# Rotary weight columns out of the shared weight buffers, and a new order of loads at the start of the latent attention

## The chip, the cores and the metric

The kernel runs on one core of one Trainium2 chip. The metric is the device time of one execution in microseconds (us), lower being better. Times are medians of several runs. The stages below are told in microseconds from the start of the profiled execution's span.

## The reference

One layer of a hybrid encoder is computed for a prompt of 1024 tokens and a sample of 32 tokens, all in 32-bit floats. What matters for the change is the mixer:

```
p = h @ w_in                                   # [q latent 384 | kv latent 256 | rotary key 32 | q_b k_b v_b | gates]
q = rms_norm(q_lat) @ w_uq                     # 8 heads of 64 + 32 columns, the 32 rotated
k_rope = apply_rope(k_r);  c_kv = rms_norm(c_kv)
k_nope, v = c_kv @ w_uk, c_kv @ w_uv           # the sample has 512 cached latents ahead of its own
o_a = softmax(mask((q_nope k_nope + q_rope k_rope) * scale)) v    # latent attention
o_b = stick-breaking attention(q_b, k_b, v_b)
merged = sigmoid(g_a) * (o_a @ w_proj_a) + sigmoid(g_b) * (o_b @ w_proj_b)
```

Then come the output projection, residual and norm, and a convolutional feed-forward part.

## The kernel before

Matrix products keep accuracy by splitting every 32-bit operand into a high part, made by ScalarE (ACT; `hi`, L65), and the difference, made by VectorE (DVE; `lo`, L68). Each product is then three matmuls on TensorE (PE): high by high, low by high and high by low (`mm3`, L72 to L74). Weights come through `wload` (L82): SyncE's queue (SP) loads a raw tile into a buffer of the tag `wr`, of which there are two, and the split writes one of two `wh` and one of two `wl` buffers. A load waits until the buffer's last readers are done.

The stages run one after the other: norm and projections, stick-breaking attention (`stage_sb`, which leaves its outputs in four DRAM tensors `ob`), latents (`stage_lat`), latent attention (`stage_mla`), merge, feed-forward up and down. Within a stage a scheduler orders the instructions of each engine, each engine executes its list in order, and SP and GpSimd (POOL) issue their DMAs in order. Inside the attention of each head pair the order of PE, ACT and DVE is written out by hand (`ORDER_A`).

`stage_lat` first makes the two key/value latent tiles (tag `lt`), then the three query latent tiles (`lat`), 128 columns each, by three products for each of eight blocks of the hidden state. Between them PE transposes the cached rotary keys, loaded by L1020, at L1024, and the key/value latents for the output at L1005, copied by ACT at L1007 and stored by POOL. Last come the rotary key columns: 32 columns of `w_in`, loaded by `wload` into a `wr` buffer, multiplied without a split at L1056, rotated with tables (L1047, L1048) and copied to the key rows by POOL (L1068). The query latents' inverse root is made by `lat_rstd`: ACT and DVE work on one row of it (an `A` tile), POOL writes it to DRAM (`lr`, L944) and reads it back as a broadcast to all partitions (`big<-lr`, L946).

`stage_mla` starts with the expansion of head pair 0: `w_uq` and `w_uk` in one `wr` tile, `w_uv` in the next. PE makes the keys (KH, KL), the values `V` (evicted by ACT at L1197 and DVE at L68), then the queries of two heads. DVE multiplies the query table `qt` by the broadcast root (L1215) and each query bank by `qt` (L1143); ACT and DVE split the result into QH and QL. The scores are L1245 to L1250. Work of another kind fills PE's gaps: `proj_b`, the projection of the stick-breaking outputs. Its operands are the four `ob` tensors, loaded in two halves (L1471) into four `A` tiles and split into `ObH` and `ObL`; its weights are `w_proj_b` tiles through `wr`. The cached latents go into the tile `VSm` (L1104) and are first read by transposes at L1341, at the start of head pair 1.

Of the kernel before, what the change touches and what calls it, by code (L numbers as in the profile page):

```python
# [8 lines left out]
F32 = mybir.dt.float32  # L9
# [8 lines left out]
P = 128  # L18
D = 1024
KT = 8  # L20
TP = 1024
# [11 lines left out]
BIG = 1056  # L33
# [3 lines left out]
HC = 528  # L37
# [7 lines left out]
class K:  # L45
# [920 lines left out]
    def stage_lat(self):  # L966
        nc, a = self.nc, self.a
# [12 lines left out]
        lp = self.tc.alloc_tile_pool(name="lt", bufs=2, reuse_waits="tile")  # L980
# [11 lines left out]
        def ckv_out():  # L992
            for k in range(2):
                self.hi(self.CPh[k], fc[k][:, :TP])
                self.lo(self.CPl[k], fc[k][:, :TP], self.CPh[k])
                nc.vector.tensor_copy(self.CN[:, k * TS : k * TS + TS], fc[k][:, TP:T])
            for t0 in (0, 4, 8):
                st = self.tl(self.At, [P, TP], F32, "A")
                for t in (t0, t0 + 2)[: 2 - t0 // 8]:
                    tr = self.bank("tr")  # L1000
                    r, n = (P, 2) if t < 8 else (TS, 1)
                    for j in range(n):
                        for k in range(2):
                            x = fc[k][:, (t + j) * P : (t + j) * P + r]
                            nc.tensor.transpose(tr[:r, j * 256 + k * P : j * 256 + k * P + P], x, self.idt)  # L1005
                    c = (t - t0) * 256
                    nc.scalar.copy(st[:r, c : c + n * 256], tr[:r, : n * 256])  # L1007
                if t0 < 8:
                    nc.gpsimd.dma_start(a["ckv_p"][0, 0, t0 * P : (t0 + 4) * P].rearrange("(j r) c -> r j c", r=P),
                                        st.rearrange("r (j c) -> r j c", j=4))  # L1010
                else:
                    nc.gpsimd.dma_start(a["ckv_s"][0, 0], st[:TS, :256])
# [15 lines left out]
        for m in range(3):  # L1028
            wh, wl = self.w_in_tile(m * P)
            g = self.gvT[:, 16 + m : 17 + m]  # L1030
            for c0, n, ps in self.mtile(wh, wl, self.Hh, self.Hl, self.BLK, KT, "mm s s"):
                c, ps = slice(c0, c0 + n), ps[:, :n]
# [5 lines left out]
                    nc.vector.tensor_tensor(sq[:, c], sq[:, c], d, ALU.add)  # L1038
            if m == 1:
                ckv_out()  # L1040
        raw = self.wload([(0, 256, a["w_in"][0, :, 640:672].rearrange("(k p) c -> p k c", p=P), 8)])
        wk = raw[:, 0:256].rearrange("p (k c) -> p k c", k=8)
        rot = self.tl(self.At, [P, BIG], F32, "big")
        cc, ss, kr, sw = (rot[:, q * TQ : q * TQ + TQ] for q in range(4))
        for q in range(4):
            r, c = slice(32 * q, 32 * q + 32), slice(TQ * q, TQ * q + TQ)
            nc.sync.dma_start(cc[r], a["k_ropek"][0:32, c])  # L1047
            nc.sync.dma_start(ss[r], a["k_ropek"][64:96, c])  # L1048
        ps = self.bank("mm")[:, :TQ]
# [15 lines left out]
        for r in halves:  # L1065
            for q in range(4):
                w = min(TQ, TP - TQ * q)
# [23 lines left out]
    def stage_mla(self):  # L1091
        nc, a = self.nc, self.a

        O = self.Op = self.tc.alloc_tile_pool(name="mlo", bufs=2, side="right", reuse_waits="tile")
# [6 lines left out]
        Vs = None  # L1101
        self.KSm = self.tl(M, [P, 2, KS], F32, "KSm")
        self.VSm = self.tl(M, [P, 5, 256], F32, "VSm")
        nc.sync.dma_start(self.VSm[:, :4], a["cache_mla_ckv"][0, 0].rearrange("(t p) c -> p t c", p=P))  # L1104

        def expansion(p, banks="mm"):

# [76 lines left out]
        def values(hf, raw, gt):  # L1184
# [3 lines left out]
            for t in range(0, 8, 2):  # L1188
# [7 lines left out]
                for q in range(2):  # L1196
# [6 lines left out]
        load_values = lambda hf: self.wload([(0, 512, a["w_uv"][0, :, hf * 256 : hf * 256 + 256]  # L1203
                                              .rearrange("(k p) c -> p k c", p=P), 2)])
        proj = self.proj_b(M, AB)
        steps, QH, QL = expansion(0, "mm s s")
        raw = load_values(0)
        steps["I"]()
# [23 lines left out]
        for p in range(4):  # L1232
# [45 lines left out]
            U = proj["U"]  # L1278
# [30 lines left out]
        for k in ks:  # L1309
            f = self.tl(self.At, [P, BIG], F32, "big")  # L1310
# [4 lines left out]
        raw = self.tl(M, [P, 2, KS], F32, "KSm")  # L1315
        raw = [self.w_proj_a(m, raw[:, m, :512]) for m in range(2)] + [self.w_proj_a(2)]
        self.w2 = raw[2]
        for m, tags in enumerate(("mm mm s", "s s")):
            h, l = self.split_proj(raw[m])
# [138 lines left out]
    def proj_b(self, M, AB):  # L1458

        nc, a = self.nc, self.a  # L1460
        HB = HC // 2
        TILES = ((0, 1), (1, 2), (3, 1), (4, 1), (5, 2), (7, 1))
        raw, w, ps, ob, done = [], [], [], [], [0, 0]

        def operands():
            h = done[0] // 6
            ob[:] = [self.tl(M, [P, 4, HC], F32R, g) for g in ("ObH", "ObL")]
            for k in range(4):
                f = self.tl(self.At, [P, BIG], F32, "big") if h else self.tl(self.At, [P, TP], F32, "A")
                f = f[:, :HC]  # L1470
                nc.sync.dma_start(f, self.obd[k][:, h * HC : h * HC + HC])  # L1471
                self.hi(ob[0][:, k], f)
                self.lo(ob[1][:, k], f, ob[0][:, k])

        def load():
            m, n = TILES[done[0] % 6]
            done[0] += 1
            raw.append(self.wload([(0, n * 512, a["w_proj_b"][0, :, m * P : (m + n) * P].rearrange("(k p) c -> p k c", p=P), 4)]))

        def high():  # L1480
            i = done[1] % 6
            done[1] += 1
            n = TILES[i][1] * 512
            w.append([x[:, :n] for x in AB[i % 3 != 1]])
            self.hi(w[-1][0], raw[0][:, :n])

        def low():
            x = raw.pop(0)
            self.lo(w[-1][1], x[:, : w[-1][1].shape[-1]], w[-1][0])

        def steps():
            for h in range(2):
                for m, i in ((m, i) for m, n in TILES for i in range(n)):
                    if i == 0:
                        wh, wl = (x.rearrange("p (k c) -> p k c", k=4) for x in w.pop(0))
                    m, d = m + i, slice(i * P, i * P + P)
                    for c0 in (0, HB):
                        c = slice(c0, c0 + HB)
                        ps.append((m, h * HC + c0, self.bank("mm")[:, :HB]))
                        for k in range(4):  # L1500
                            self.mm3(ps[-1][2], wh[:, k, d], wl[:, k, d], ob[0][:, k, c], ob[1][:, k, c], k == 0, k == 3)
                            yield

        def store():
            m, c0, x = ps.pop(0)
            g = self.tl(self.At, [P, 512], F32, "nat")[:, :HB]
            nc.scalar.copy(g, x)
            nc.gpsimd.dma_start(self.pbd[m, :, c0 : c0 + HB], g)

        step = steps()  # L1510
        return dict(O=operands, U=load, W=high, w=low, f=lambda: next(step), G=store)


    def natural(self, facc, lhs, ws, first, done=None, sample=None, tiles=range(8)):
# [825 lines left out]
```

## Time and profile before

| | |
|---|---|
| median of 3 runs | 1711.94 us (1710.65 to 1712.59) |
| profiled execution | 1715.34 us, span 1713.6 us |
| granted TensorE clock | 0.995 |
| PE, DVE, ACT, POOL busy | 98%, 72%, 57%, 16% of the span |
| latents, head pair 0 begins | about 512 to 594, then from 595 us |

In the rows of a timeline the columns are start, duration, engine, line, operation, tiles written and read, and shapes; in brackets stand the engine's idle time before the instruction and what ended it. `x3` after a row means that three neighbours are merged into it. The waits view gives, for an engine and a line, what it waited for: sum in us, times, longest. A row of groups gives busy time and mean duration (ns) of the instructions of one form. A row of DMA issues gives the count, the size of each and the median time from issue to landing. Matmuls overlap in their pipeline, so the time of one counts from start to start.

### The profile page before, as it was taken

To read this page: it belongs to the slowest core of one execution; us is meant where nothing else is said; L and a number is where in the kernel's file an instruction comes from. 1 tells how busy PE (TensorE), PEld (TensorE's weight loads), DVE (VectorE), ACT (ScalarE), POOL (GpSimd) and SP (SyncE) were. 2 spreads that over 40 slices of the span, in tenths; PEclk is the share of its full clock that TensorE was granted. 3 is DMA by queue.
4 is the path that set the end of the run, shared out by engine and by line. 5 is a ranking of instruction groups with operands and counts; after the bars stand their busy time and mean duration, and the time that the engine had idled before them with its cause. 6 is when DMAs were issued, how large, how long until landed. Compare 5 with 4: busy or idle time off the path is not lost. (4 is left out here: it accounts for less than half of the span.)

```text
span 1713.6 us, 29725 instructions
## 1 busy us (share of the span) xinstructions
PE 1674.5 (98%) x11526; PEld 1524.6 (89%) x11526; DVE 1236.0 (72%) x2065; ACT 979.1 (57%) x1902; POOL 277.6 (16%) x530
## 2 busy tenths in 40 slices
PE   6999999999999999999999999999999999999998
PEld 3899999999999889988889789999999999977886
DVE  4596595593782488877775779887787787788456
ACT  4495595693773467777673376544444444545442
POOL 2211111111110121111000121221121111110013
PEclk8999999999999999999999999999999999999999
DMA  9244342333441231222174631523323333697753
GB/s 328 83 117 121 94 131 78 98 107 86 140 123 48 89 101 53 67 59 74 52 272 150 191 123 36 168 93 130 130 93 130 130 105 130 224 332 248 230 151 120
DMA packets 169805, 224.33 MB, mean 131 GB/s; under 512 B 13326, under 2 KB 115872, under 8 KB 169664
## 3 DMA queue, kind: packets, MB, share of 16 engines
q1 hardware_dynamic: 153216, 177.11, 32.9%
q0 software_dynamic: 16224, 45.24, 7.6%
q8 instruction: 90, 1.47, 0.4%
q14 instruction: 51, 0.42, 0.1%
q10 hardware_dynamic: 224, 0.09, 0.0%
HBM read 170.34 MB, written 51.25 MB: 129 GB/s over the span
## 5 line engine op out<-in xcount | busy, mean ns | idle before, releaser
L65 ACT ACTIVATE wh<-wr 128x1024 fp32r<-128x1024 f32 (+5 forms) x153 | 130.6, 861 | 247.9 <-PE s L1794 82.2
L68 DVE TENSOR_TENSOR wl<-wr,wh 128x1024 fp32r<-128x1024 f32 (+5 forms) x153 | 150.4, 989 | 137.8 <-ACT wh L65 135.3
L72 PE MATMUL mm<-hh,wh 128*128 128x352 f32 x688 | 229.5, 334 | 2.2 <-ACT nat L870 2.2
L73 PE MATMUL mm<-hl,wh 128*128 128x352 f32 x688 | 223.9, 325 | 0.4 <-DVE hl L300 0.3
L74 PE MATMUL mm<-hh,wl 128*128 128x352 f32 x688 | 223.2, 324 | 0.0
L72 PEld LDWEIGHTS mm<-hh,wh 128*128 128x128 f32 x688 | 129.8, 189 | 10.2 <-ACT nat L870 4.1
L73 PEld LDWEIGHTS mm<-hl,wh 128*128 128x128 f32 x688 | 129.8, 189 | 3.5 <-DVE hl L300 2.1
L74 PEld LDWEIGHTS mm<-hh,wl 128*128 128x128 f32 x688 | 129.9, 189 | 0.4 <-issue 0.4
L1795 PE MATMUL s<-T,wl 128*128 128x256 f32 (+1 forms) x328 | 93.6, 285 | 0.0
L1794 PE MATMUL s<-T,wh 128*128 128x256 f32 (+1 forms) x328 | 93.4, 285 | 0.0
L1793 PE MATMUL s<-T,wh 128*128 128x256 f32 (+1 forms) x328 | 93.3, 284 | 0.0
L1934 DVE SCALAR_TENSOR_TENSOR u<-u,c,u 128x1058 f32<-128x1058 f32 x68 | 87.0, 1317 | 2.0 <-ACT u L1931 0.7
L611 PE MATMUL tr<-c,A 128*128 128x128 f32 x576 | 83.5, 273 | 0.5 <-DVE A L727 0.3
L1793 PE MATMUL tr<-T,wh 128*128 128x272 f32 (+1 forms) x272 | 77.8, 286 | 0.0
L1795 PE MATMUL tr<-T,wl 128*128 128x272 f32 (+1 forms) x272 | 77.6, 285 | 0.1
L1794 PE MATMUL tr<-T,wh 128*128 128x272 f32 (+1 forms) x272 | 77.3, 284 | 0.0
L68 DVE TENSOR_TENSOR wl<-S,wh 128x1024 fp32r<-128x1024 f32 x40 | 48.9, 1224 | 36.7 <-ACT wh L65 35.5
L611 PEld LDWEIGHTS tr<-c,A 128*128 128x128 f32 x576 | 67.8, 140 | 6.3 <-ACT A L550 1.6
L1795 PE MATMUL mm<-T,wl 128*128 128x256 f32 (+1 forms) x256 | 72.9, 286 | 0.3 <-DVE wl L68 0.2
L1793 PE MATMUL mm<-T,wh 128*128 128x256 f32 (+1 forms) x256 | 73.0, 285 | 0.0
L1794 PE MATMUL mm<-T,wh 128*128 128x272 f32 (+1 forms) x256 | 72.7, 284 | 0.0
L68 DVE TENSOR_TENSOR PTl<-tr,PTh 128x512 fp32r<-128x512 f32 x96 | 64.6, 684 | 8.2 <-ACT PTh L65 7.9
(694 smaller groups left out, 5444.1 us busy)
## 6 DMA issues: line engine op xcount, KB each, us to landing
wr<-in_w_ada_dram SPq DMA_DIRECT2D x48, 512.0 KB, 4.3
wr<-in_w_up_dram SPq DMA_DIRECT2D x44, 512.0 KB, 3.9
dr<-in_w_down_dram SPq DMA_DIRECT2D x43, 512.0 KB, 5.1
wr<-in_w_in_dram SPq DMA_DIRECT2D x33, 512.0 KB, 4.8
wr<-gdn SPq DMA_DIRECT2D x30, 512.0 KB, 4.9
gdn<-u POOLq DMA_DIRECT2D x23, 512.0 KB, 5.4
gd<-nat POOLq DMA_DIRECT2D x48, 176.0 KB, 2.1
t<-gd SPq DMA_DIRECT2D x16, 528.0 KB, 5.5
```

What stands on the lines that cost most here:

```text
L65: self.nc.scalar.activation(out, in_, AF.Identity, scale=scale)
L68: return self.nc.vector.tensor_tensor(out, full, hi.bitcast(F32), ALU.subtract)
L72: m(ps, lh, rh, start=start, stop=False)
L73: m(ps, lh, rl, start=False, stop=False)
L74: self.pe = m(ps, ll, rh, start=False, stop=stop).ins
L611: self.nc.tensor.transpose(tr[:, (2 * s + q) * P : (2 * s + q + 1) * P], at[q][:, b * P : b * P + P], self.idt)
L1793: m(ps[:, :n], w[0][:, k], x[0][:, k, c], start=first and k == 0, stop=False, skip_group_check=True)
L1794: m(ps[:, :n], w[0][:, k], x[1][:, k, c], start=False, stop=False, skip_group_check=True)
L1795: i = m(ps[:, :n], w[1][:, k], x[0][:, k, c], start=False, stop=k == 3, skip_group_check=True)
L1934: nc.vector.scalar_tensor_tensor(y, u[:, w : w + YW], self.cvT[:, w, cc : cc + 1], y, ALU.mult, ALU.add)
```

## The change

The rotary columns get a tile of their own, `wk`, in the stage's own pool `lt`, in place of a `wr` buffer. In `stage_mla` the loads of the first halves of the stick-breaking outputs become a function of their own (`fetch`, key `P`), called before the expansion; the cached latents' load is written behind it, with the condition that it is not issued before the last of those four loads. `operands` splits what `fetch` has loaded, and calls it where that has not happened, as for the second halves.

```diff
-        raw = self.wload([(0, 256, a["w_in"][0, :, 640:672].rearrange("(k p) c -> p k c", p=P), 8)])
-        wk = raw[:, 0:256].rearrange("p (k c) -> p k c", k=8)
+        wk = lp.tile([P, 8, 32], F32, name=self.nm("wk"), bufs=1)
+        nc.sync.dma_start(wk, a["w_in"][0, :, 640:672].rearrange("(k p) c -> p k c", p=P))
...
-        nc.sync.dma_start(self.VSm[:, :4], a["cache_mla_ckv"][0, 0].rearrange("(t p) c -> p t c", p=P))
...
         proj = self.proj_b(M, AB)
+        proj["P"]()
+        with self.tc.issue_after(self.fetched):
+            nc.sync.dma_start(self.VSm[:, :4], a["cache_mla_ckv"][0, 0].rearrange("(t p) c -> p t c", p=P))
         steps, QH, QL = expansion(0, "mm s s")
...
-        raw, w, ps, ob, done = [], [], [], [], [0, 0]
-
-        def operands():
+        raw, w, ps, ob, fs, done = [], [], [], [], [], [0, 0]
+
+        def fetch():
             h = done[0] // 6
-            ob[:] = [self.tl(M, [P, 4, HC], F32R, g) for g in ("ObH", "ObL")]
             for k in range(4):
                 f = self.tl(self.At, [P, BIG], F32, "big") if h else self.tl(self.At, [P, TP], F32, "A")
-                f = f[:, :HC]
-                nc.sync.dma_start(f, self.obd[k][:, h * HC : h * HC + HC])
+                fs.append(f[:, :HC])
+                self.fetched = nc.sync.dma_start(fs[-1], self.obd[k][:, h * HC : h * HC + HC]).ins
+
+        def operands():
+            ob[:] = [self.tl(M, [P, 4, HC], F32R, g) for g in ("ObH", "ObL")]
+            if not fs:
+                fetch()
+            for k in range(4):
+                f = fs.pop(0)
                 self.hi(ob[0][:, k], f)
                 self.lo(ob[1][:, k], f, ob[0][:, k])
...
-        return dict(O=operands, U=load, W=high, w=low, f=lambda: next(step), G=store)
+        return dict(P=fetch, O=operands, U=load, W=high, w=low, f=lambda: next(step), G=store)
```

In the built program the instructions of both kernels are the same in number. What differs in their order: on SP, the rotary columns' load stands ahead of the last query latent tile's, `w_uq` and `w_uk` ahead of the cached rotary keys, and the four `ob` loads ahead of the cached latents; on ACT and DVE, the splits of `ob` stand earlier among the copies of `V`; on PE, the transposes at L1024 stand two products later; on POOL, one copy of key rows (L1225) stands one store earlier. Everything from head pair 0's scores on stands in the same order.

## The prediction, made before the changed kernel was run

> **What bounds the kernel now.** I read the page's first part, then the waits of PE in the stretch that holds the change (540 to 625 us), then SP's queue there, then the timelines of ACT, DVE and PE row by row.
>
> ```profile
> PE 1674.5 (98%) x11526; PEld 1524.6 (89%) x11526; DVE 1236.0 (72%) x2065; ACT 979.1 (57%) x1902; POOL 277.6 (16%) x530
> ```
> ```profile
> PE tr L1005 <- ACT A L1007: 1.2, 1, 1.2
> PE s L72 <- DVE V L68: 0.9, 1, 0.9
> PE s L1250 <- DVE QL L68: 0.9, 1, 0.9
> PE s L1245 <- DVE big L1143: 0.4, 1, 0.4
> PE s L1245 <- ACT QH L65: 0.3, 1, 0.3
> ```
>
> PE is busy for 98% of the span, so an edit gains only where PE stands still, and loses only where it makes PE stand still. The second fence is the waits view for PE between 540 and 625 us (sum, count, longest): five waits, 3.7 us together. Nothing else in this stretch stops PE, so these five are the whole prize. None names a DMA. The next rows show that a DMA stands behind every one: SP's queue first.
>
> ```profile
> 550.06 0.37 SPq L82 DMA_DIRECT2D wr<-in_w_in_dram  x1
> 551.03 0.92 SPq L1020 DMA_DIRECT2D nat<-in_cache_mla_krope_dram  x2
> 570.46 0.39 SPq L82 DMA_DIRECT2D wr<-in_w_uq_dram  x1
> 578.10 0.37 SPq L82 DMA_DIRECT2D wr<-in_w_uv_dram  x1
> 588.74 0.37 SPq L82 DMA_DIRECT2D wr<-in_w_proj_b_dram  x1
> 594.81 0.37 SPq L1104 DMA_DIRECT2D VSm<-in_cache_mla_ckv_dram  x1
> 595.27 0.46 SPq L82 DMA_DIRECT2D wr<-in_w_proj_b_dram  x1
> 595.83 1.95 SPq L1471 DMA_DIRECT2D A<-ob  x4
> ```
> ```profile
> 573.52 0.69 ACT L65 ACTIVATE wh<-wr 128x576 fp32r<-128x576 f32 x1 [3.96 <-DMA wr<-in_w_uq_dram]
> 574.89 1.07 ACT L1007 COPY A<-tr 128x512 f32<-128x512 f32 x2
> 601.37 0.39 ACT L1197 ACTIVATE V<-mm 128x256 fp32r<-128x256 f32 x1
> 604.49 0.65 ACT L65 ACTIVATE ObH<-A 128x528 fp32r<-128x528 f32 x1 [1.93 <-DMA A<-ob]
> 607.67 0.65 ACT L65 ACTIVATE ObH<-A 128x528 fp32r<-128x528 f32 x1 [1.41 <-DMA A<-ob]
> ```
>
> The load at 550.06 brings the rotary columns into one of the two `wr` buffers, where they stay until the rotary products (L1056) end at 594.8. Everything else goes through the other buffer, one at a time: `w_uq` at 570.46, `w_uv` at 578.10, the first `w_proj_b` tile at 588.74. The second `w_proj_b` tile needs the rotary buffer (595.27). The cached latents' load (594.81) needs memory that the same products read. The four loads of the stick-breaking outputs (`ob`) stand behind both. ACT is in order: it waits 3.96 us for `w_uq`, then 1.93 and 1.41 us for `ob`, with the copies that PE needs queued behind.
>
> **Part 1: the rotary columns leave the `wr` pool.** In the built program their load stands ahead of the last query-latent tile's and waits only for attention products that are over before the latents begin; `w_uq` and `w_uk` take the place at 550.06, so the 3.96 us wait goes. What is late next is ACT's `wh` buffer, which the products of the second query-latent tile read until just before these transposes:
>
> ```profile
> 572.31 1.03 PE L1005 MATMUL tr<-c,lt 128*128 128x128 f32 x8
> 575.53 1.15 PE L1005 MATMUL tr<-c,lt 128*128 128x128 f32 x8 [1.22 <-ACT A L1007]
> ```
>
> So ACT's split starts at 572.4 instead of 573.52, and the copy at 574.89, three instructions behind it, 1.1 us earlier. PE waited 1.22 us for that copy and then waits 0.1. Worth 1.1 us (bounds 0 and 1.2).
>
> What is put in the way: 416 KB (288 + 128) instead of 128 KB are now queued right ahead of the two key loads (L1020), whose transposes PE runs here:
>
> ```profile
> 554.36 0.63 PE L1024 MATMUL tr<-c,nat 128*128 128x128 f32 x4
> ```
> ```profile
> wr<-in_w_uq_dram SPq DMA_DIRECT2D x1, 288.0 KB, 3.0
> A<-ob SPq DMA_DIRECT2D x4, 264.0 KB, 9.5
> big<-lr POOLq DMA_DIRECT2D x1, 528.0 KB, 8.1
> big<-lr POOLq DMA_DIRECT2D x1, 528.0 KB, 4.2
> ```
>
> The `w_uq` load took 3.0 us to land, so from 550.06 it lands at 553.1. The key loads were issued by 551.95 and landed by 554.36, within 2.4 us. At worst they begin when `w_uq` has landed: 555.5, or 1.1 us late. The new PE order sets the transposes two products later, 0.3 us at the 0.17 of the products further below (27 from 609.52 to 613.96), so PE loses at most 0.8. At best nothing changes, as the rotary load of 128 KB also stood ahead before. I take 0.3, nearer the free end, since the key loads are issued a microsecond behind either way. The Trainium skill ("DMA: Bandwidth & Descriptors", section on queues, rings and completion order) says that each DMA engine consumes one queue's descriptors in ring order. By that rule the cost is the 0.8 end and the sum below is 3.8 us instead of 4.3; no view here separates the two.
>
> **Part 2: the `ob` loads go ahead.** The second `w_proj_b` tile now waits for DVE's split of `w_uv`. In the kernel before, the load at 588.74 waits for that same split, so the tile leaves at 588.74 less the 1.1 of part 1, at 587.6. Three `ob` loads follow at once, done by 589.5; their buffers were last read by the latents' output stores, done long before. At the crowded 9.5 us they land by 599.0. The fourth waits until the 4 KB root row has been written, which is what POOL also waits for here:
>
> ```profile
> 596.17 0.57 POOL L946 DMA_DIRECT2D big<-lr  x1 [1.32 <-DMA lr<-A]
> ```
>
> That makes it 595.1. The broadcast `big<-lr` (528 KB) and the cached latents (512 KB) then travel beside it, instead of those two, three more `ob` loads and a `w_proj_b` tile. The two `big<-lr` rows give the price of a crowd: 4.2 us alone, 8.1 within it. With the lighter crowd I take the middle, 6, so the fourth lands at 601. The cached latents are late by nothing: their first reader is L1341, in the second head pair. The loads behind them on SP wait for later splits anyway. On POOL one copy of key rows (L1225) moves ahead of one store; the second head's scores read it, after the whole first head.
>
> Now DVE, the engine behind four of the five waits:
>
> ```profile
> 600.91 0.42 DVE L68 TENSOR_TENSOR V<-mm,V 128x256 fp32r<-128x256 f32 x1
> 610.24 1.25 DVE L1215 TENSOR_TENSOR qt<-qt,big 128x1056 f32<-128x1056 f32 x1
> ```
> ```profile
> L68 DVE TENSOR_TENSOR ObL<-A,ObH 128x528 fp32r<-128x528 f32 x4 | 2.8, 706 | 2.0 <-ACT ObH L65 1.8
> L1143 DVE TENSOR_TENSOR big<-s,qt 128x352 f32<-128x352 f32 x4 | 2.1, 518 | 0.0
> L68 DVE TENSOR_TENSOR KL<-A,KH 64x1024 fp32r<-64x1024 f32 x1 | 1.2, 1223 | 0.0
> ```
>
> From the first V difference to the query table's product (L1215) DVE takes 9.3 us for eight V differences (0.42) and four ObL (0.71): 6.2 us of work, the rest waiting for ACT. ACT's own part is eight copies (0.39), four ObH (0.65) and a weight split of an ObH's length, 6.4 us begun before DVE's, so it keeps pace. Starting at 600.91 - 1.1 = 599.8, the table product starts at 606.0 instead of 610.24: 4.2 earlier. It also needs `big<-lr`: 595.1 + 6 = 601 (603.2 at 8.1).
>
> ```profile
> 608.11 0.49 PE L1074 MATMUL tr<-c,big 128*128 128x128 f32 x3
> 609.52 0.40 PE L72 MATMUL s<-lat,wh 128*128 128x352 f32 x1 [0.93 <-DVE V L68]
> 613.96 0.32 PE L74 MATMUL s<-lat,wl 128*128 128x352 f32 x1
> 614.54 0.39 PE L1245 MATMUL s<-KH,QH 128*128 128x256 f32 x1 [0.26 <-ACT QH L65]
> 616.03 0.39 PE L1250 MATMUL s<-KH,QL 128*128 128x256 f32 x1 [0.90 <-DVE QL L68]
> 616.80 0.39 PE L1245 MATMUL s<-KH,QH 128*128 128x256 f32 x1 [0.38 <-DVE big L1143]
> 617.66 0.44 PE L1245 MATMUL s<-KH,QH 128*128 128x384 f32 x1
> 618.42 0.28 PE L72 MATMUL mm<-ObH,wh 128*128 128x264 f32 x1
> ```
>
> First stall: three transposes at a tenth each (eight took 1.03) would let the second head's queries start at 608.5; they start at 609.52, held by the seventh of the eight V differences. All eight are now done by 606.0, before PE comes by at 607.4. Worth 1.0.
>
> Second stall: the last query product starts at 613.96, the next could at 614.1. Three score groups follow, and the filler starts at 618.42: 4.3 us. The third group (384 columns) took 0.76 to the next start; at that pace 256 + 256 + 384 columns take 1.8. So 2.5 are lost (1.5 by the waits view alone, since a stall also shows the pipeline's fill). In the changed kernel PE reaches the scores at about 612. DVE's queue up to QL is, from 606.0: table 1.25, weight split 0.7 (as ObL), three products with the table 1.55, KL 1.2, QL of the same length 1.2, so 611.9. It comes just in time and this wait goes. The second head's products with the table then wait only for PE, so the bank of the third score group is free as PE arrives. I take 2.5, bounds 1.0 and 2.8.
>
> **The sum.** 1.1 - 0.3 + 1.0 + 2.5 = 4.3 us. Nothing later gives it back in the trace: PE, DVE and ACT start the first head pair with the same distances to each other, and PE stays the bound. The profiled execution took 1715.34 us (span 1713.6, 1.7 around it); it would take 1711.0. The median of the runs is 1711.94, 3.4 below that execution, and becomes 1707.6. About 0.2% (3.4 us) is what a measurement of this kernel can tell from no change.
>
> **Rivals.**
> *A, only part arrives.* ACT and DVE get rid of the DMA waits, but QL and the table products still end behind PE. DVE's sum of 611.9 against PE's 612 has no slack, which speaks for it; that 612 is PE's earliest, with no stall on the way, speaks against. The scores then give 1.0 instead of 2.5 and the key loads cost 0.8: 1.1 - 0.8 + 1.0 + 1.0 = 2.3, or 1709.6.
> *B, the fourth `ob` load takes the place.* Issued at 595.1, at 9.5 us it lands at 604.6, and ACT is due there by 602.5 (two V copies and three ObH, 2.7 us, behind the first V). V copies are queued behind, and the table product moves by 2.1 to 608.1: 2.1 ahead of before. Less 0.3 at L1024, 1.8 us: 1710.1. Against it: the 9.5 came with 1.3 MB more in flight (three `ob` loads and a `w_proj_b` tile).
> *C, slower.* The new ACT order has two ObH splits right behind the first V copy, ahead of the other seven; before, two more V copies came first. Were the first `ob` loads not to leave earlier (if a buffer's wait held them to 596), the second would land at 596.2 + 9.5 = 605.7, and DVE then still has 5.8 us of V and ObL work: table product at 611.5, 1.3 later than before, with 0.3 at L1024: 1713.5. It becomes a loss from a landing of 604.4 on. Against it: none of their waits ends after 589.
> *D, nothing moves*, because PE's stalls are other than named: 1711.9.
>
> **How the numbers follow.** Forecast 0.70, A 0.14, B 0.07, C 0.06, D 0.03. The forecast's own bounds: 5.0 us at most (1.2 + 1.0 + 2.8, keys free), that is 1706.9; 3.0 at least. The lowest of the three runs before lay 1.3 us below their median, so the low end is 1705.6. The high end takes in A, and B with 0.7 of the same scatter: 1710.8. Faster by over 0.2% is nearly all of the forecast and a little of A, 0.70; slower by over 0.2% at most C, 0.06; within 0.2% the rest, 0.24.
>
> **What would show it.** Right: `w_uq` issued near 550, no DMA wait on ACT's splits, `ob` loads near 588, the five waits of PE down to under 0.6 us, the filler that started at 618.42 near 614. Wrong: L1024 waiting for its load past 555; ACT waiting for the fourth `ob` load; PE still waiting for QL. A gain under 2 us with all waits gone would mean that PE's time is set elsewhere.

## The result, and the profile after

The changed kernel takes 1708.04 us (median of 22 runs, 1705.33 to 1711.15), the kernel before 1712.35 (22 runs, 1709.24 to 1716.29): a ratio of 0.9977 (95% interval 0.9971 to 0.9983), 4.3 us less. Measured twice more it came to 0.9973 (0.9963 to 0.9983) and 0.9975 (0.9965 to 0.9985). The forecast was 1707.6 us.

The first fence is the page's line of busy times. Then come the waits of PE from 540 to 625 us, one row where the kernel before had five, and SP's queue.

```profile
PE 1671.6 (98%) x11526; PEld 1524.1 (89%) x11526; DVE 1234.8 (72%) x2065; ACT 978.3 (57%) x1902; POOL 274.6 (16%) x530
```
```profile
PE tr L1024 <- DMA nat<-in_cache_mla_krope_dram: 0.3, 1, 0.3
```
```profile
549.74 0.37 SPq L82 DMA_DIRECT2D wr<-in_w_uq_dram  x1
550.16 0.48 SPq L82 DMA_DIRECT2D wr<-in_w_uk_dram  x1
550.96 0.92 SPq L1020 DMA_DIRECT2D nat<-in_cache_mla_krope_dram  x2
570.32 0.38 SPq L82 DMA_DIRECT2D wr<-in_w_uv_dram  x1
576.80 10.98 SPq L82 DMA_DIRECT2D wr<-in_w_proj_b_dram  x2
587.87 7.23 SPq L1472 DMA_DIRECT2D A<-ob  x4
595.19 0.39 SPq L1207 DMA_DIRECT2D VSm<-in_cache_mla_ckv_dram  x1
```

`w_uq` leaves at 549.74 instead of 570.46, the `ob` loads begin at 587.87 instead of 595.83, and the fourth (the row of four ends at 595.10) goes just ahead of the cached latents. The timelines of ACT and DVE show what follows.

```profile
572.22 0.69 ACT L65 ACTIVATE wh<-wr 128x576 fp32r<-128x576 f32 x1 [2.78 <-PE s L73]
598.55 1.17 ACT L65 ACTIVATE ObH<-A 128x528 fp32r<-128x528 f32 x2
600.56 1.18 ACT L65 ACTIVATE ObH<-A 128x528 fp32r<-128x528 f32 x2
```
```profile
599.56 0.42 DVE L68 TENSOR_TENSOR V<-mm,V 128x256 fp32r<-128x256 f32 x1
604.69 1.25 DVE L1217 TENSOR_TENSOR qt<-qt,big 128x1056 f32<-128x1056 f32 x1
609.22 1.21 DVE L68 TENSOR_TENSOR QL<-big,QH 128x1024 fp32r<-128x1024 f32 x1
610.71 0.52 DVE L1142 TENSOR_TENSOR big<-s,qt 128x352 f32<-128x352 f32 x1
611.15 0.51 DVE L1142 TENSOR_TENSOR big<-mm,qt 128x352 f32<-128x352 f32 x1
611.65 0.53 DVE L1142 TENSOR_TENSOR big<-s,qt 128x352 f32<-128x352 f32 x1
```

ACT's split of `w_uq` no longer waits for a DMA but for PE's release of `wh`, and the four ObH splits have no bracket: their data is there. The query table's product (now L1217) starts 5.13 us behind the first V difference instead of 9.33. On PE:

```profile
554.58 0.63 PE L1024 MATMUL tr<-c,nat 128*128 128x128 f32 x4 [0.33 <-DMA nat<-in_cache_mla_krope_dram]
572.19 1.03 PE L1005 MATMUL tr<-c,lt 128*128 128x128 f32 x8
574.24 1.14 PE L1005 MATMUL tr<-c,lt 128*128 128x128 f32 x8
606.76 0.49 PE L1074 MATMUL tr<-c,big 128*128 128x128 f32 x3
607.01 0.41 PE L72 MATMUL s<-lat,wh 128*128 128x352 f32 x1
611.29 0.32 PE L74 MATMUL s<-lat,wl 128*128 128x352 f32 x1
611.45 0.28 PE L1247 MATMUL s<-KH,QH 128*128 128x256 f32 x1
611.93 0.28 PE L1247 MATMUL s<-KH,QH 128*128 128x256 f32 x1
612.41 0.34 PE L1247 MATMUL s<-KH,QH 128*128 128x384 f32 x1
613.06 0.29 PE L72 MATMUL mm<-ObH,wh 128*128 128x264 f32 x1
```

From the first to the second row of L1005 PE needs 2.05 us, before 3.22; from the three transposes at L1074 to the second head's queries 0.25, before 1.41; from the last query product to the filler 1.77, before 4.46. To compare stretches between kernels I took the same matmuls in each trace, by their number in order of start (3602, 3735, 3887 and 4199 of 11,526, which in the first profile of before start at 549, 570, 590 and 632 us). Three profiles of each kernel (one of each comes from the first pair, the others from the experiments below):

| stretch of PE, us | before | changed | difference of means |
|---|---|---|---|
| keys transposed, 549 to 570 | 20.95, 20.62, 20.70 | 21.15, 20.98, 21.13 | +0.3 |
| latents' transposes, 570 to 590 | 20.06, 19.78, 19.58 | 18.84, 18.85, 18.84 | -1.0 |
| values, queries, scores, 590 to 632 | 41.95, 41.89, 42.10 | 37.91, 37.92, 37.93 | -4.0 |
| sum | 82.96, 82.29, 82.38 | 77.90, 77.75, 77.90 | -4.7 |

The first pair of profiles differs by 7.1 us in all (1715.34 and 1708.21). What goes beyond this stretch differs from execution to execution: the three of before took 1715.34, 1711.82 and 1710.66 us.

### The profile page after: what moved, and what is told of

It reads as the page before. It is cut to its first block, busy times and chain, and to the rows that moved or that the text cites. A ratio compares the mean times of both kernels' runs of the same rounds, so it can differ in the third digit from the quotient of the medians.

```text
span 1706.4 us, 29725 instructions
## 1 busy us (share of the span) xinstructions
PE 1671.6 (98%) x11526; PEld 1524.1 (89%) x11526; DVE 1234.8 (72%) x2065; ACT 978.3 (57%) x1902; POOL 274.6 (16%) x530
```

## The experiments

**The columns alone.** Only the first part of the diff; the cached latents' load keeps its place ahead of `ob`.

```diff
+        wk = lp.tile([P, 8, 32], F32, name=self.nm("wk"), bufs=1)
+        nc.sync.dma_start(wk, a["w_in"][0, :, 640:672].rearrange("(k p) c -> p k c", p=P))
```

> The kernel before with only the rotary columns in a tile of their own; the cached latents' load stays ahead of the ob loads. My theory (two parts, and the ob loads' departure is what matters in the second): PE's 1.22 us wait at L1005 goes, 0.2 us is lost at L1024, and no more, because the ob loads still stand behind a load that waits for the rotary products, so they leave from about 594 on, the second lands at about 603, just short of the 604.4 at which a loss begins, and the query table product starts near 609. PE still waits for V, QL and the score banks, 2.0 to 2.5 us together. Gain 0.9 us (0.3 to 1.8), about 0.05%. Rival 1 (the tile alone does it all, since it also lets the second w_proj_b tile leave early and thins the crowd): gain 4 to 5 us, 0.25 to 0.3%, the filler behind the scores starts near 613. Rival 2 (late ob loads in front of the copies of V cost): a loss of 0 to 1 us.

1709.74 us, ratio 0.9979 (0.9970 to 0.9988). By the times that is a gain of 3.6 us (2.1 to 5.1). The profile shows less where the change acts: from 549 to 632 us PE takes 80.4 us, 2.2 less than the mean of before. That is more than my 0.9 and less than rival 1. Its rows on SP, ACT and DVE:

```profile
594.81 0.37 SPq L1104 DMA_DIRECT2D VSm<-in_cache_mla_ckv_dram  x1
595.27 1.95 SPq L1471 DMA_DIRECT2D A<-ob  x4
```
```profile
599.89 1.17 ACT L65 ACTIVATE ObH<-A 128x528 fp32r<-128x528 f32 x2
604.28 0.65 ACT L65 ACTIVATE ObH<-A 128x528 fp32r<-128x528 f32 x1 [2.27 <-DMA A<-ob]
```
```profile
600.90 0.42 DVE L68 TENSOR_TENSOR V<-mm,V 128x256 fp32r<-128x256 f32 x1
608.55 1.25 DVE L1215 TENSOR_TENSOR qt<-qt,big 128x1056 f32<-128x1056 f32 x1
```

The `ob` loads do leave as late as before. But ACT splits the first two without a wait at 599.89, 4.6 us after the first was issued; only the third makes it wait. I had priced the second load at 9.5 us, the median of the row of four. The view knows the landing of the third and the fourth alone (8.8 and 10.2 us), so this was never a price of the second. So rival 2, the slower case of the prediction, starts from a wrong price: with the splits early and the loads late DVE gains 0.8 to 1.8 us (7.65 against 9.33, 8.47 and 9.49 in the profiles of before) instead of losing any. Part of that may come from the second `w_proj_b` tile, which is no longer in flight beside `ob`; with it, in the next run, the distance is 7.91.

**The order alone.** The changed kernel with the columns back in a `wr` buffer.

```diff
-        wk = lp.tile([P, 8, 32], F32, name=self.nm("wk"), bufs=1)
-        nc.sync.dma_start(wk, a["w_in"][0, :, 640:672].rearrange("(k p) c -> p k c", p=P))
+        raw = self.wload([(0, 256, a["w_in"][0, :, 640:672].rearrange("(k p) c -> p k c", p=P), 8)])
+        wk = raw[:, 0:256].rearrange("p (k c) -> p k c", k=8)
```

> The changed kernel with the rotary columns back in a wr buffer; only the order of the loads is changed. My theory: PE's 1.2 us wait at L1005 stays. The ob loads stand behind the second w_proj_b tile, which waits for the rotary buffer until 594.8, so they leave from 595.3 on, as late as before; the second lands at 603 to 604, the table product starts near 610, and the sum is 0 (between a gain of 1.0 and a loss of 1.3 us), within 0.1% of before. Rival 1 (the order of the loads brings the gain by itself, being ahead of the cached latents): gain 3 to 4 us, 0.2%. Rival 2 (the slower case of the prediction): loss of 1.0 to 1.6 us.

1711.51 us, ratio 0.9995 (0.9986 to 1.0004): no change that can be told, as expected. The wait at L1005 stays (0.9 us), and `ob` leaves behind the tile that waits:

```profile
586.46 6.89 SPq L82 DMA_DIRECT2D wr<-in_w_proj_b_dram  x2
593.45 1.90 SPq L1472 DMA_DIRECT2D A<-ob  x4
595.40 0.48 SPq L1207 DMA_DIRECT2D VSm<-in_cache_mla_ckv_dram  x1
```

The table product comes 7.91 us behind the first V difference, and PE takes 81.7 us from 549 to 632, 0.9 less than the mean of before. The parts alone give 2.2 and 0.9, together 4.7: the second needs the first, which frees the queue ahead of it. In this profile, as in one of the three of before, the granted clock fell behind the scores, which cost 0.8 us (last section). Without it the three numbers are about 1.9, 1.4 and 4.4, so some 1 us is what the parts gain only together.

**Both kernels again**, for the scatter of single profiles.

> The changed kernel once more, for a second profile. If the change's effect ends in the stretch of 540 to 625 us, the ends of PE's matmuls lie about 5 us ahead of before at 625 us in this profile too, and what is gained or lost after 700 us (2 us in the first pair of profiles) differs from execution to execution. If the change acts on the later stages, the same 2 us come back at the same places (847, 890 and 1500 to 1540 us). Median near 1708.

> The kernel before once more, for a second profile: the same five waits of PE (3.7 us in 540 to 625 us), and against the first profile of before shifts of up to 2 us after 700 us, if the later shifts are scatter between executions; shifts under 0.3 us, if they are not.

1707.88 and 1711.82 us. Of the five waits four came again; the one for V did not (the table product comes 8.47 us behind the first V difference here). The effect ends at 632 us: there the second profiles are 3.6 us apart (the changed one began the stretch 0.9 us later), and 3.9 at the end. Of the 1.8 us that the first pair gains after 700 us, 1.1 us stand between the two profiles of before as well; they belong to the first execution, not to the change.

**The cached latents from ACT's queue**, at their old place, beside the columns' tile.

```diff
-        nc.sync.dma_start(self.VSm[:, :4], ...
+        nc.scalar.dma_start(self.VSm[:, :4], ...
```

> The kernel before with the rotary columns in a tile of their own (as in the run of the columns alone) and the cached latents' load issued from ACT's queue, at its old place in the program, so that nothing that waits for the rotary products stands ahead of the ob loads on SP. The number of bytes in flight stays what it was. My theory (the second part of the gain is the place in SP's in-order queue, behind a waiting load, and nothing else): the first three ob loads leave near 588, the fourth near 595, the table product comes within 5.5 us of the first V difference (7.7 with the columns alone, 5.1 in the changed kernel), PE's waits for QL and the score banks go, and the ends of PE's matmuls gain what the changed kernel gains, 4.5 to 5.2 us, 2.3 us more than the columns alone; ratio near 0.9975. Rival (the cached latents' 512 KB beside the ob loads are what delays them): the table product stays near 7.5 us and the gain near 2.3 us.

1708.95 us, ratio 0.9981 (0.9972 to 0.9991); PE takes 79.0 us from 549 to 632, 3.5 less than before, and the table product comes at 6.04. That lies between theory and rival.

```profile
594.08 0.40 ACTq L1104 DMA_DIRECT2D VSm<-in_cache_mla_ckv_dram  x1
602.35 0.65 ACT L65 ACTIVATE ObH<-A 128x528 fp32r<-128x528 f32 x1 [0.82 <-DMA A<-ob]
```
```profile
588.48 7.41 SPq L1471 DMA_DIRECT2D A<-ob  x4
```

Three `ob` loads leave at 588.48, as in the changed kernel. The fourth leaves with 512 KB of cached latents just ahead of it on another queue, lands in 6.8 us instead of 2.7, and ACT waits for it. From 590 to 632 us PE takes 40.0 us with the columns alone (mean of two profiles), 38.6 here and 37.9 in the changed kernel: of these 2.1 us about 1.4 are the place behind a waiting load in SP's queue. The other 0.7 are lost with the cached latents ahead of the fourth load. My "nothing else" was wrong. This split rests on one profile here, and the two with the columns alone differ by 0.5 us. The times don't separate the three kernels (0.9979, 0.9981 and 0.9977 of before).

**The rotary keys from ACT's queue**, in the changed kernel.

```diff
-            nc.sync.dma_start(kr.rearrange(...
+            nc.scalar.dma_start(kr.rearrange(...
```

> The changed kernel with the two loads of the cached rotary keys (L1020) issued from ACT's queue instead of SP's, where 416 KB stand ahead of them. If those 416 KB hold them up (ring order), PE's wait at L1024 (0.3 us in the first profile of the changed kernel, its transposes 0.4 us later than in three profiles without the change) goes, and 0.3 to 0.5 us are gained there. If the wait is the keys' own time to land (2.9 us), it stays. Elsewhere nothing moves; the total is within scatter of the changed kernel either way.

```profile
549.26 0.39 ACTq L1020 DMA_DIRECT2D nat<-in_cache_mla_krope_dram  x1
549.78 0.43 ACTq L1020 DMA_DIRECT2D nat<-in_cache_mla_krope_dram  x1
553.44 0.63 PE L1024 MATMUL tr<-c,nat 128*128 128x128 f32 x4 [0.63 <-DMA nat<-in_cache_mla_krope_dram]
```

1707.22 us, a single run. The wait stays, at 0.63 us; the keys took 3.6 us to land with nothing ahead of them on their queue, against 3.0 behind the 416 KB on SP's queue in the first profile of the changed kernel. So a queue of their own doesn't bring them sooner. The Trainium skill ("DMA: Bandwidth & Descriptors", section "Issuing engines are not separate DMA queues") says that the queues of all issuing engines run on the same DMA engines and interleave; this trace agrees in so far as the other queue gained nothing (3.6 against 3.0 us).

**More work on DVE.** In the changed kernel the query table is multiplied by 1.0 two or five times more behind its product, and nothing else changes.

```diff
+        for _ in range(2):      # or 5
+            nc.vector.tensor_scalar(qt, qt, 1.0, None, ALU.mult)
```

> The changed kernel with two more products of the query table by 1.0 on DVE, right behind the table product, so that all that follows on DVE is later and nothing else changes (no DMA, no other engine). From the rows of two scalings (0.35 us for 256, 0.49 for 512 columns) each should take some 0.75 us, 1.5 together. My theory: in the changed kernel DVE's QL ends 1.3 us before PE asks for it, so only about 0.2 us (0 to 0.6) is lost at the scores. Rival (DVE's queue comes just in time, as the prediction's sum had it): 1.5 us are lost.

> The same with five more products, 3.75 us on DVE. My theory: beyond the 1.3 us of slack each us on DVE costs one us, so 2.4 us (1.9 to 3.2) are lost at the scores, PE waits for QL and the score banks as in the kernel before, and the ratio to before goes from 0.9975 to near 0.999. Rival (no slack): 3.75 us. Rival 2 (PE's stall at the scores was made by something other than DVE's queue): under 1 us.

DVE's QL is 1.56 and 3.86 us later, and PE's stretch from 590 to 632 us grows by 1.37 and 4.34. With two products a single run takes 1709.28 us. With five it is 1713.24 us and a ratio of 1.0007 (0.9998 to 1.0016): the whole gain is gone. My 1.3 us of slack was wrong, the rival without slack right. The rows with two products show where the slack went:

```profile
610.86 0.53 DVE L1142 TENSOR_TENSOR big<-s,qt 128x352 f32<-128x352 f32 x1
611.73 0.51 DVE L1142 TENSOR_TENSOR big<-s,qt 128x352 f32<-128x352 f32 x1
```
```profile
611.44 0.39 PE L1249 MATMUL s<-KH,QH 128*128 128x256 f32 x1 [0.38 <-DVE big L1142]
612.30 0.44 PE L1249 MATMUL s<-KH,QH 128*128 128x384 f32 x1
```

The second and third score groups start 0.05 and 0.06 us after the first and third of the second head's table products have ended (611.39 and 612.24): they need those banks, and the products stand behind QL in DVE's queue. In the changed kernel the third product ends at 612.18 and the third group starts at 612.41, 0.17 us more than the 0.06 that the hand-over takes. So QL has 1.3 us to spare, but what is queued behind it has 0.17. Put that way, all profiles but three lie on one line. Its last column is the time that PE would take if each us by which QL comes later than in the changed kernel, less those 0.17, cost one us:

| kernel | QL behind first V difference, us | PE, 590 to 632 us | 37.91 + (QL - 9.66 - 0.17) |
|---|---|---|---|
| changed (three profiles) | 9.66 | 37.91 to 37.93 | |
| cached latents from ACT | 10.57 | 38.63 | 38.65 |
| two more products | 11.22 | 39.28 | 39.30 |
| columns alone (two profiles) | 11.72, 12.18 | 39.78, 40.26 | 39.80, 40.26 |
| before (first, third) | 13.86, 14.02 | 41.95, 42.10 | 41.94, 42.10 |
| order alone | 12.44 | 41.33 | 40.52 |
| before (second) | 12.99 | 41.89 | 41.07 |
| five more products | 13.52 | 42.25 | 41.60 |

The last three lie 0.65 to 0.82 us above it. They are the three in which the granted clock fell behind the stalls (the last section).

**The weights behind the keys.** In the changed kernel `w_uq` and `w_uk` are held until the keys' loads are issued.

```diff
+            with self.tc.issue_after(self.keyload):
                 raw = self.wload([
...
```

> The changed kernel with the loads of w_uq and w_uk held until the two loads of the cached rotary keys have been issued, so that the 416 KB stand behind the keys instead of ahead of them; the transposes at L1024 go back to their old place, two products earlier. The run with the keys on ACT's queue left the wait in place (0.63 us), so a place in SP's queue is not what holds the keys up. Theory 1 (the 416 KB in flight share the DMA engines with the keys, whatever the queue; those that start first are served first): the keys land in the 3.05 us that they have in the kernel before, no wait at L1024, and PE takes 0.3 to 0.6 us less from 549 to 570 us than in the profiles of the changed kernel (20.98 and 21.15). Theory 2 (bytes that start behind the keys slow them as much): a wait of 0.3 to 1.0 us stays. No other stretch changes; the total is within 0.1% of the changed kernel.

> The changed kernel a third time, on the chip of the run above, for a third profile: a wait at L1024 between 0 and 1.0 us, PE's stretch from 590 to 632 us the same as in the two profiles before it (37.9 us) within 0.1 us, median near 1708.

1707.70 us, 0.9970 (0.9959 to 0.9980), and 1707.86 us, 0.9975: not to be told apart. PE takes 21.01 us from 549 to 570, against 21.15, 20.98 and 21.13 in the changed kernel. The wait for the keys is gone from the view, as theory 1 has it, but the time is not shorter. PE still stands still for 0.17 us at L1024. The view puts that down to DVE's L942, which can't be the cause: in the second profile of before the transposes started at 552.27, 0.27 us before that instruction ended.

This stretch scatters more than three profiles show. In the five other runs with the weights ahead of the keys on SP's queue it takes 21.02 to 21.80 us, though the two doses on DVE, which gave both of these ends, do not touch it. So one profile can't price the order of these loads to better than some tenths, and why PE takes 0.3 us or more beyond before there stays open.

**A third profile of before and a second of the columns alone**, for the fall of the clock.

> The kernel before a third time. In its second profile, in the run with the order alone and in the one with five more products, the granted clock falls to 0.50 for 3.4 us right behind the stalls at the scores (about 614.5 to 618.5 us) and the 15 filler products cost 1.5 us more; in the first profile of before and in the run with the columns alone the same stalls leave it at 1.00; in no profile without these stalls does it fall there. If the fall depends on how the stalls lie in time and not on the kernel, it comes or not in this profile, with PE's stretch from 549 to 632 us between 81.5 and 83.5 us; if the first profile was the exception, it comes again.

> The kernel before with the rotary columns alone, a second time, for the same question: PE's stretch from 549 to 632 us 80.4 us without a fall of the clock behind the scores, 81.9 us with one. The three gains of its first profile (1.1 us at L1005, the wait for V gone, the table product 7.7 us behind the first V difference) come again in either case.

1710.66 and 1709.41 us; the clock stays at 1.00 behind the scores in both. PE's stretch is 82.4 and 80.0 us. The fall comes and goes with the execution; the gains of the columns alone came again (wait at L1005 and wait for V gone, table product at 7.19), though the wait for V was also missing in one profile of before.

## Why the prediction was right

**The sum.** Forecast 1.1 - 0.3 + 1.0 + 2.5 = 4.3 us; the profiles give 1.0 - 0.3 + 4.0 = 4.7, the times 4.3 (2.9 to 5.0 from the interval). Of the 4.0 the first pair has 1.2 at the first stall (forecast 1.0) and 2.7 at the second (forecast 2.5). "These five are the whole prize" was wrong: the waits view gives 3.7 us, and in the first pair their places gave 5.3 (20.06 - 18.84 and 41.95 - 37.91). The distance from start to start, which the prediction used for the second stall, came closer than the waits view, which gave less than PE lost.

**Part 1.** `w_uq` left at 549.74 and ACT's split started at 572.22, released by PE (forecast 572.4). The gain was 1.0 (forecast 1.1). The cost at L1024 was 0.3 (forecast 0.3) in the three profiles of the changed kernel; in the five other runs with these loads in this order it was 0.3 to 1.0, so that this term fits so well is in part luck. Ring order as the prediction priced it did not show: the transposes started at 554.58, not at 555.5, and neither a queue of their own nor a place ahead of the weights made this stretch of PE shorter by more than 0.1 us. What the cost is made of was not found.

**Part 2, the loads.** They left as forecast (587.87 and 595.1). `big<-lr` landed in 6.2 us (forecast 6), the fourth `ob` load in 2.7 (forecast 6): with the cached latents ahead of it, in the run from ACT's queue, it took 6.8.

**Part 2, DVE.** Here a term was mis-sized. I added durations, 6.2 us for twelve differences; on DVE neighbours overlap (a V difference lasts 0.42 us, and the next instruction starts 0.33 behind it), and the twelve took 5.13 from start to start. The table product came 1.1 us sooner than my step had it, and mostly by that QL ended at 610.43, not 611.9.

**The second stall.** "It comes just in time" was right, but not for the reason given. "The second head's products with the table then wait only for PE" failed: they wait for DVE, behind QL, and their third has the 0.17 us. Had DVE really needed 6.2 us, about 0.9 us of the gain would have been lost, by the line of the table above. The two mistakes cancelled, which was luck.

**The rivals.** A, only part arrives: its waits were gone, but its condition, no slack, is what the two doses found. B: no wait for the fourth load in the changed kernel; with the cached latents in its way it waits 0.82 us, so the mechanism is real and smaller than priced. C: its situation (late `ob`, early splits) was run twice, and neither was slower (0.9979 and 0.9995 of before). Its price, 9.5 us for the second of four loads, was that of the third and the fourth. D fell with the first row of waits.

**Where the gain comes from** is told less well by the prediction's two parts than by the experiments: the columns alone bring 1.0 at L1005, lose 0.5 at L1024 and bring 1.7 to 2.2 of what I had put down to the order of the `ob` loads (two profiles).

## What to carry to other kernels

A DMA that waits for its buffer holds up all that stands behind it in its queue (the `ob` loads left at 595.27 behind one, and three of them at 588.48 without it), so ask of each late load what the one ahead of it waits for. Here two such holders had to go for the whole gain, and taking away the second alone gained nothing that the times could tell. A median over several loads is no price for the first of them. Time a chain on an in-order engine from start to start, and look past the instruction that a consumer waits for to the ones queued behind it that free the banks: the slack is the smallest of them. A small dose of work in that chain measures the slack in one run.

## What the runs showed of the hardware that was not expected

Behind the stalls at the scores the granted clock of TensorE fell to 0.50 in some executions. The windows view of the second profile of before (columns: stretch, its length, busy time of PE, PEld, DVE, ACT and POOL, granted clock, share of the DMA engines, GB/s), and below it the same stretches of the third:

```profile
612.00:615.00 3.00, 1.75 (x9) 1.16 (x10) 2.86 (x9) 0.79 (x2) 1.28 (x3) 1.00 0.50 94
615.00:618.00 3.00, 3.00 (x15) 3.00 (x15) 2.91 (x4) 1.78 (x7) 0.00 (x0) 0.50 0.00 0
```
```profile
612.00:615.00 3.00, 1.64 (x8) 1.05 (x8) 2.90 (x8) 0.81 (x1) 1.89 (x4) 1.00 0.63 131
615.00:618.00 3.00, 2.96 (x21) 2.61 (x21) 2.89 (x7) 2.80 (x8) 0.00 (x0) 1.00 0.00 0
```

With PE busy for 1.75 of 3 us the clock halved for 3.4 us (0.51, 0.50, 0.50 and 0.78 in the four stretches of 1 us from 615), and PE passed 15 matmuls where it passed 21 in the third profile; with 1.64 of 3 us it did not halve. The fall happened in one of three profiles of before, in that of the order alone and in that with five more products, never at this place in one without these stalls; it cost 0.65 to 0.82 us net in the table above.

Stretches of 3 us taken at will do not tell the cases apart; the clock's own steps do. In each of the 14 profiles any two changes of the granted clock lie a whole number of steps of 3.4133 us apart, to 0.03 us. In the second of before they are at 24.52, 27.94, 31.34, 34.76, 615.02, 618.44 and 1707.30 us. Carried on to the stalls, this grid gives the stretch at whose end the clock could change. Here are those of the second of before (the fall follows), the order alone (it follows), the columns alone and the first of before (it does not):

```profile
611.61:615.02 3.41, 2.00 (x12) 1.28 (x11) 3.27 (x10) 1.20 (x2) 1.63 (x4) 1.00 0.51 101
610.83:614.24 3.41, 2.07 (x12) 1.47 (x11) 3.28 (x9) 1.35 (x2) 2.21 (x4) 1.00 0.57 120
611.65:615.06 3.41, 2.24 (x14) 1.89 (x12) 3.29 (x7) 2.12 (x2) 2.40 (x5) 1.00 0.58 145
612.56:615.97 3.41, 2.31 (x13) 1.85 (x12) 3.35 (x5) 2.01 (x2) 3.38 (x6) 1.00 0.72 161
```

PE was busy for 1.90 to 2.07 us in the three grid stretches that a fall followed, and for 2.24 or more in those at the scores of all other profiles. Each profile of before has some 3.41 us at the stalls with only 1.8 of work; whether a stretch of the grid takes in so little depends on where the grid lies. That is how the same stalls bring a fall in one execution and none in the next. Busy time is not the whole rule: near the start of the third profile of before the stretch from 19.41 us has 1.92, and no fall followed.

The Trainium skill ("TensorE: Matmul & The Clock Gate", Part 1) states a half rate after at least one idle window of some 3.4 us, the window running freely. Half rate, length and the free-running window agree; an idle window was not needed here, PE being busy for 1.90 to 2.07 of 3.41 us. So removing a stall can also remove a slow phase that follows it in some executions, which the one profile that I predicted from did not show.
